# Closing the sample's 32 tokens in two column halves, behind the last prompt tile's closing multiply

## The chip, the core and the metric

The kernel runs on one core of one Trainium2 chip. The metric is the time of one execution on the device in microseconds (us); less is better. The core's engines work side by side and wait for each other through semaphores: PE (TensorE, matrix products), DVE (VectorE), ACT (ScalarE), POOL (GpSimd), and SP, which issues most of the DMA transfers between HBM and SBUF, the on-chip memory. SBUF has 128 partitions; an address here is a byte offset within a partition.

## The reference: what is computed

Two groups of tokens go through two mixer layers with shared weights: 4096 prompt frames and 32 sample frames of width 1024. Each layer adds a gated mixer output to the residual x, and a final RMSNorm closes both groups:

```python
def trunk(x, c, conv_st, gla_st, pool_st, pos0, ...):
    for l in range(DEPTH):                       # DEPTH = 2
        h = rms_norm(x, norm_g[l]) * (1.0 + scale[:, None, :]) + shift[:, None, :]
        if l % 2 == 0:
            y, cb, gs = even_mixer(h, ...)       # conv branch and gated linear recurrence, w_out
        else:
            y, pb = pool_mixer(h, ...)           # trailing means, gate, then @ w_out
        x = x + gate[:, None, :] * y
    return rms_norm(x, final_g), ...

def rms_norm(x, g):
    y = x * lax.rsqrt(jnp.mean(x * x, axis=-1, keepdims=True) + EPS)
    return y * g
```

The change concerns the last two steps for the 32 sample frames: `x + gate * y` and the final `rms_norm`.

## The kernel before

**Tiles and stages.** The 4128 tokens are cut into 11 blocks: ten of 384 prompt tokens and a last one of 256 prompt and 32 sample tokens. The program goes through stages, each over all blocks: A (first input projection, conv branch; matmul results in `psA`), B (recurrence branch; `psv`, `psg`, `psk`, `psq`), C (first output projection; `psC`), D (second input projection and pooling; `psD`), E (second output projection and final norm; `psE`). Intermediate results go through HBM between the stages.

**Float32 products in three passes.** Every float32 operand is split into a high part and a low part of the rounded type f32r, and a product is the sum of three matmuls (`PASS`). In stages A and D, and for `psg`, `psk`, `psq` of B, `gemm_B` (L162) holds a 128x128 piece of the weights `w` in PE and streams the activation tile `h[k]` (384 columns, or 288 in the last block) past it: 8 tiles k times 3 passes are 24 matmuls for one result tile. The profile's names give the streamed operand first: `psD<-h,w_du` streams `h`, `psE<-w_e,op` streams the weights `w_e`, with `op` held. In `psv`, `psC` and `psE` the weights are streamed and the activations are held.

**Where the tiles lie.** SBUF is handed out by pools, one behind the other, each as large as its tags need: `cst`, `wp`, `stg`, `sm`, then `hp` (whose 12 buffers hold the tiles `h`, `hB`, `hC`), then the pools of the stages (`A`; `B` and `B1`; `xp`; `C`; `D`; `E`, which takes over the place of `hp` too). The pools `A2`, `CE` and `X0` are opened with `side="right"` and placed from the end of SBUF. `sm` holds the small per-token sums (`ss`, `r`, `rt1`, ...). Each tile's buffer begins at a multiple of 32 bytes. Two tags of activations lie outside `hp`: the tiles k = 6 and 7 of every block in stage A (pool `A`, `split_h` with `(ap_, 3)`), and the tiles k = 6 and 7 of blocks 1 to 9 in stage B (pool `B1`, tag `hx`, L147 and L1010). Block 0 in stage B has all eight in `hp`.

**The end of the program.** In stage E, `add` and `finish` (L1404) close the prompt tiles in pairs: DVE adds the products to `xE`, ACT squares the row with a running sum, POOL makes the reciprocal root in two instructions (`rstd_pool`, L213), and the rest of `finish`, a DVE multiply by root and weight (L1413) and the output DMA on SP's queue (L1414), comes when `flush()` is called. Stage E runs in an order tied by `keep_in_program_order` for the matmuls, ACT's `act` and the DVE instructions inside `pin`; instructions outside these are placed by the scheduler. After the last pair, a loop over two column halves nh does the sample: 16 matmuls into `psES`, `sum_S` (L208: an ACT copy and a DVE add), a DVE multiply by the gate `gS` (L1509), a DVE add to `xS` (L1510); `flush()` stands at the end of the loop body. Then `finish` runs once over all 1024 columns of `xS`.

Of the kernel before, what the change touches and what calls it, by code (L numbers as in the profile page):

```python
# [8 lines left out]
F32 = mybir.dt.float32  # L9
F32R = mybir.dt.float32r  # L10
BF16 = mybir.dt.bfloat16
U8 = mybir.dt.uint8
AF = mybir.ActivationFunctionType
ALU = mybir.AluOpType
PSUM = bass.MemoryType.PSUM

P = 128
D = 1024
# [12 lines left out]
def trunk(  # L31
# [8 lines left out]
    nc = tc.nc  # L40
    L = x_prompt.shape[1]
    NS = x_sample.shape[1]
# [26 lines left out]
    LB = blocks[-1]  # L69
# [4 lines left out]
    def rows(ap_p, ap_s, blk, c0, n, seq):  # L74
        if seq:
            return ap_s[0, 0:n, :]
        return ap_p[0, blk.start + c0:blk.start + c0 + n, :]
# [5 lines left out]
    sm = ctx.enter_context(tc.tile_pool(name="sm", bufs=3))  # L83
# [6 lines left out]
    def mm(shape, name):  # L90
        t = pp.tile(shape, F32, tag=f"m{turn['m']}", name=name, bufs=2)
        turn["m"] = (turn["m"] + 1) % 3
        return t
# [67 lines left out]
    def pin(ins):  # L161
        if PIN["dve"]:  # L162
            tc.keep_in_program_order(ins)

    def mmul(*args, **kw):
        ins = nc.tensor.matmul(*args, **kw)  # L166
        if PIN["on"]:
            tc.keep_in_program_order(ins)
# [6 lines left out]
    def act(*args, **kw):  # L175
        ins = nc.scalar.activation(*args, **kw)  # L176
        if PIN["act"]:
            tc.keep_in_program_order(ins)
# [34 lines left out]
    def rstd_pool(out, ss, n, m, inv, name):  # L213

        t = sm.tile([P, m], F32, tag=f"rt{m}", name=f"rt_{name}")
        nc.gpsimd.tensor_scalar(out=t[:n], in0=ss, scalar1=inv, scalar2=EPS, op0=ALU.mult, op1=ALU.add)  # L216
        nc.gpsimd.tensor_tensor(out=out, in0=t[:n], in1=mhalf[:n, 0:m], op=ALU.pow)  # L217
# [214 lines left out]
    with tc.tile_pool(name="A", bufs=2, reuse_waits="tile") as ap_:  # L432
# [166 lines left out]
        for blk in blocks:  # L599
# [4 lines left out]
            for idx, (kind, c, col) in enumerate(order):  # L604
# [14 lines left out]
                elif kind == "val":  # L619
# [8 lines left out]
                    for (c0, m, seq) in blk.segs:  # L628
                        if seq:
# [3 lines left out]
                                                       in1=av[:, c0:c0 + m], op0=ALU.add, op1=ALU.mult)  # L633
# [103 lines left out]
    with ExitStack() as bctx:  # L737
# [7 lines left out]
        for r in range(4):  # L745
            t = bp.tile([P, 2, P], F32, name=f"attm{r}")
# [160 lines left out]
        for blk in blocks:  # L907
# [25 lines left out]
            for (i0, i1, m) in ([(0, nsub, P)] if not blk.last else [(i, i + 1, sb[1]) for i, sb in enumerate(blk.subs)]):  # L933
# [3 lines left out]
                                        in1=lrs[:m, i0:i1, 0, :].bitcast(F32), op=ALU.subtract)  # L937
# [31 lines left out]
            for j in range(2):  # L969
# [5 lines left out]
                                                 op0=ALU.add, op1=ALU.min)  # L975
# [12 lines left out]
            for i, (c0, m, seq) in enumerate(blk.subs):  # L988
# [3 lines left out]
                                        in1=la.to_broadcast([P, 2, m]), op=ALU.subtract)  # L992
# [93 lines left out]
    with tc.tile_pool(name="C", bufs=2, reuse_waits="tile") as cp:  # L1086
# [37 lines left out]
        for blk in blocks:  # L1124
# [10 lines left out]
            for u, (i, nh) in enumerate(units):  # L1135
# [7 lines left out]
                t = cp.tile([P, 512], F32, tag="pg", name=f"pgC{blk.i}_{i}{nh}")  # L1143
                if seq:
                    sum_S(t[:m], ps, m)
                pg_ins = nc.vector.tensor_tensor(out=t[:m], in0=t[:m] if seq else ps[:m], in1=grow[:m, seq, cols],
                                                 op=ALU.mult)
                nc.vector.tensor_tensor(out=xt[:m, cols], in0=t[:m], in1=xt[:m, cols], op=ALU.add)
                if nh == 1:
                    nc.sync.dma_start(x1D[blk.i][i], xt[:m])  # L1150
                    junk = cp.tile([P, 512], F32, tag="pg", name=f"junkC{blk.i}_{i}").bitcast(BF16)
# [120 lines left out]
    with tc.tile_pool(name="D", bufs=2, reuse_waits="tile") as dp:  # L1272
# [3 lines left out]
        for blk in blocks:  # L1276
# [3 lines left out]
            for idx, (kind, j) in enumerate(dord):  # L1280
# [6 lines left out]
                if kind == "u":  # L1287
# [14 lines left out]
                    while step < wn:  # L1302
                        t = dp.tile([P, UW], F32, tag="s", name=f"s{blk.i}_{j}_{step}")
# [6 lines left out]
                                                   in1=u[:, PP:off], op0=ALU.mult, op1=ALU.subtract)  # L1310
# [4 lines left out]
                else:  # L1315
# [3 lines left out]
                    for (c0, m, seq) in blk.segs:  # L1319
                        a = PP + c0 + (PP if seq else 0)  # L1320
                        nc.vector.scalar_tensor_tensor(out=y1[:, c0:c0 + m], in0=pt[:, a:a + m], scalar=gbs[:, j:j + 1],  # L1321
                                                       in1=sgt[:, c0:c0 + m], op0=ALU.add, op1=ALU.mult)
# [14 lines left out]
    with tc.tile_pool(name="E", bufs=2, reuse_waits="tile") as ep:  # L1337
# [4 lines left out]
        fg = ep.tile([P, D], F32, name="fg", bufs=1)  # L1342
# [19 lines left out]
        def load_xE(p):  # L1362
            xs = []
            for r, (b, i, c0) in enumerate(pairs[p]):
                xt = ep.tile([P, D], F32, tag="x", name=f"xE{p}_{r}", bufs=4)
                (nc.sync if p else nc.gpsimd).dma_start(xt, x1D[b.i][i])
                xs.append(xt)
            return xs
# [28 lines left out]
        def prod(ps, left, i, first):  # L1397
            m = 0
            for k in range(4):
                for (hi, wi) in PASS:  # L1400
                    mmul(ps, left.ops[i][:, hi, k, :], wE[PROD[i], k // 2][:, wi, k % 2, :],
                         start=bool(first) and m == 0, stop=m == 11,
                         skip_group_check=not first)
                    m += 1  # L1404

        def finish(xt, n, name, dst):
            junk = ep.tile([P, D], BF16, tag="junk", name=f"junk{name}", bufs=1)
            ss = sm.tile([P, 1], F32, tag="ss", name=f"ss{name}")
            act(junk[:n], xt[:n], AF.Square, accum_out=ss[:n])
            r = sm.tile([P, 1], F32, tag="r", name=f"r{name}")  # L1410
            rstd_pool(r[:n], ss[:n], n, 1, 1.0 / D, name)
            yield
            pin(nc.vector.scalar_tensor_tensor(out=xt[:n], in0=xt[:n], scalar=r[:n], in1=fg[:n], op0=ALU.mult, op1=ALU.mult))  # L1413
            nc.sync.dma_start(dst, xt[:n])  # L1414
# [3 lines left out]
        def flush():  # L1418
            for g in ends:
                list(g)  # L1420
            ends.clear()

        H = (slice(0, 512), slice(512, 1024))
# [18 lines left out]
        for p in range(len(pairs)):  # L1442
            more = p + 1 < len(pairs)
            nxt = nxs = None
            if p > 0 and more:
                nxt, nxs = Left(p + 1), load_xE(p + 1)
            x1, x2 = xs
            bank = [mm([P, 512], f"psE{p}_{q}") for q in range(3)]

            def add(x, h, ps):  # L1450
                pin(nc.vector.tensor_tensor(out=x[:, H[h]], in0=ps, in1=x[:, H[h]], op=ALU.add))  # L1451


            for i, (q, first, adds) in enumerate(((0, 1, (x1, 0)), (1, 1, (x1, 0)), (0, 0, (x1, 1)), (2, 1, (x2, 1)),
                                                  (0, 0, (x2, 1)), (2, 0, (x1, 1)), (0, 0, (x2, 0)))):
                prod(bank[q], cur, i, first)
                add(*adds, bank[q])
                flush()
                if i >= 5:
                    b, _, c0 = pairs[p][i - 5]  # L1460
                    ends.append(finish(xs[i - 5], P, f"E{p}_{i - 5}", rows(y_prompt, y_sample, b, c0, P, 0)))
                    next(ends[-1])
                if p == 0:

                    if i < 4:
                        cur.make(i + 3)
                    if i == 0:
                        lateE.pop(0)(), lateE.pop(0)()
                        nxt = Left(1)
                        nc.sync.dma_start(fg, final_g.partition_broadcast(P))  # L1470
                    if i in (2, 3):
                        lateE.pop(0)()
                    if i == 3:
                        nxs = load_xE(1)
                    for j in ((), (), (), (0,), (1, 2), (3,), (4,))[i]:
                        nxt.make(j)
                    continue
                if p == 1 and i < 2:
                    cur.make(i + 5)
                if more:  # L1480
                    nxt.make(i)
                else:
                    load_S(i)
                    if i == 6:
                        load_S(7)
                if not more and i == 2:

                    ysr = stg.tile([P, KT, MH], F32, tag="st", name="ys")
                    nc.sync.dma_start(ysr, y1D[LB.i][:, :, LB.np:LB.n])
                    hS = ep.tile([P, KT, 3 * MH], F32R, tag="op", name="hS", bufs=8)  # L1490
                    nc.scalar.activation(hS[:, :, 0:MH], ysr, AF.Copy)
                    for q in (1, 2):
                        nc.vector.tensor_tensor(out=hS[:, :, q * MH:(q + 1) * MH], in0=ysr,
                                                in1=hS[:, :, 0:MH].bitcast(F32), op=ALU.subtract)
                    xS = ep.tile([P, D], F32, tag="x", name="xS", bufs=4)
                    nc.sync.dma_start(xS[:NS], x1D[LB.i][len(LB.subs) - 1])
                    gS = ep.tile([P, D], F32, tag="x", name="gS", bufs=4)
                    nc.sync.dma_start(gS[:NS], gateD[1][1, :].partition_broadcast(NS))
            cur, xs = nxt, nxs
        for nh in range(2):  # L1500
            ps = mm([P, 512], f"psES{nh}")
            m = 0
            for k in range(KT):
                for wi in range(2):
                    mmul(ps[:3 * MH], hS[:, k, :], wS[nh, k // 2][:, wi, k % 2, :], start=(m == 0), stop=(m == 2 * KT - 1))
                    m += 1
            t = ep.tile([P, 512], F32, tag="S", name=f"tS{nh}", bufs=4)
            sum_S(t[:NS], ps, NS)
            nc.vector.tensor_tensor(out=t[:NS], in0=t[:NS], in1=gS[:NS, H[nh]], op=ALU.mult)  # L1509
            nc.vector.tensor_tensor(out=xS[:NS, H[nh]], in0=t[:NS], in1=xS[:NS, H[nh]], op=ALU.add)  # L1510
            flush()
        list(finish(xS, NS, "ES", rows(y_prompt, y_sample, LB, LB.np, NS, 1)))


_INS = ["x_prompt", "x_sample", "c_prompt", "c_sample", "state_conv", "state_gla", "state_pool",
# [29 lines left out]
```

## Time and profile before

| | |
|---|---|
| median of 3 runs | 2864.99 us (2864.03 to 2866.5) |
| the profiled execution's own time | 2866.98 us |
| its span | 2865.3 us, in which PE is busy 2812.4 us, DVE 1959.7 us, ACT 1023.9 us |
| granted PE clock, mean | 0.994 |
| stages, by the first matmul of each | A from 62 us, B from 639 us, C from 1346 us, D from 1779 us, E from 2535 us |
| last matmul starts, last DVE instruction starts, last DMA is issued | 2854.24 us, 2861.12 us, 2862.42 us |

Times within a profile count from the span's start. The span covers the instructions that the profiler recorded; the execution's own time is 1.68 us longer. "x24" behind a row is a count of instructions; the duration of such a row reaches from the start of its first instruction to the end of its last.

### The profile page before, as it was taken

What the parts mean: (1) busy time and instruction counts of PE and PEld (TensorE: products, weight loads), DVE (VectorE), ACT (ScalarE), POOL (GpSimd) and SP (SyncE); (2) the same over time, 40 slices, a digit from 0 to 9 for tenths busy, and PEclk for the clock granted to TensorE, in tenths of its full rate; (3) what the DMA queues carried; (4) which work ended last, traced back from release to release, by engine and by line L of the source; (5) the groups of instructions that cost most, each with busy time, mean ns of one, the idle gap of its engine ahead of it and who ended that gap; (6) DMA issues with size and microseconds to landing.
All of it is one profiled execution on the core that took longest, in us unless ns stands there. A gap on an engine that the chain in (4) does not pass through costs nothing. (4 is left out here: it accounts for less than half of the span.)

```text
span 2865.3 us, 43285 instructions
## 1 busy us (share of the span) xinstructions
PE 2812.4 (98%) x16593; PEld 2612.3 (91%) x16593; DVE 1959.7 (68%) x3907; ACT 1023.9 (36%) x2137; POOL 247.1 (9%) x492
## 2 busy tenths in 40 slices
PE   7999999999999999998999999999999999999998
PEld 5999999999999999997878887999999999988886
DVE  4997886888878888886866674533333333577776
ACT  5434334334334334334232224422222323343333
POOL 1110000000000000011111110001111110000000
PEclk9999999999999999999999999999999999999999
DMA  8523323233111111115455554312222221365544
GB/s 290 156 87 106 105 95 106 78 112 91 59 51 49 45 45 57 48 47 185 168 195 184 191 194 139 125 62 69 73 71 71 69 71 51 116 204 176 164 159 155
DMA packets 249667, 323.70 MB, mean 113 GB/s; under 512 B 18793, under 2 KB 198907, under 8 KB 248947
## 3 DMA queue, kind: packets, MB, share of 16 engines
q1 hardware_dynamic: 248635, 318.78, 34.2%
q8 instruction: 130, 2.13, 0.3%
q0 software_dynamic: 704, 2.11, 0.2%
q14 instruction: 78, 0.64, 0.1%
q10 hardware_dynamic: 120, 0.04, 0.0%
HBM read 211.21 MB, written 109.65 MB: 112 GB/s over the span
## 5 line engine op out<-in xcount | busy, mean ns | idle before, releaser
L166 PE MATMUL psC<-w_c,hC 128*128 128x512 f32 (+1 forms) x1568 | 377.0, 397 | 0.0
L166 PE MATMUL psD<-h,w_du 128*128 128x384 f32 (+1 forms) x2112 | 376.6, 332 | 0.1
L166 PE MATMUL psD<-h,w_dg 128*128 128x384 f32 (+1 forms) x2112 | 376.4, 332 | 0.0
L417 DVE SCALAR_TENSOR_TENSOR co<-g,cwt,co 128x384 f32<-128x384 f32 (+1 forms) x660 | 370.1, 605 | 4.9
L166 PEld LDWEIGHTS psD<-h,w_du 128*128 128x128 f32 x2112 | 357.8, 188 | 1.0 <-DVE h L152 0.4
L166 PEld LDWEIGHTS psD<-h,w_dg 128*128 128x128 f32 x2112 | 357.8, 188 | 0.5
L166 PEld LDWEIGHTS psC<-w_c,hC 128*128 128x128 f32 (+1 forms) x1568 | 292.9, 189 | 60.7
L417 DVE SCALAR_TENSOR_TENSOR coB<-glB,cwt,coB 128x384 f32<-128x384 f32 x600 | 333.1, 610 | 0.0
L166 PE MATMUL psE<-w_e,op 128*128 128x512 f32 x1344 | 307.6, 391 | 4.2 <-DVE xE L1451 2.4
L166 PEld LDWEIGHTS psE<-w_e,op 128*128 128x128 f32 x1344 | 253.0, 189 | 58.6 <-issue 3.2
L166 PE MATMUL psv<-w_wv,hB 128*128 128x264 f32 (+1 forms) x1568 | 207.3, 288 | 2.0 <-ACT vt L891 2.0
L166 PEld LDWEIGHTS psv<-w_wv,hB 128*128 128x128 f32 (+1 forms) x1568 | 195.0, 188 | 5.0 <-ACT vt L891 2.4
L166 PE MATMUL psg<-hB,w_bg 128*128 128x384 f32 (+1 forms) x1056 | 189.5, 336 | 3.2 <-ACT vt L891 1.5
L166 PE MATMUL psA<-h,w_aglu 128*128 128x384 f32 (+1 forms) x1056 | 190.4, 333 | 0.2
L166 PE MATMUL psA<-h,w_aval 128*128 128x384 f32 (+1 forms) x1056 | 189.1, 333 | 0.0
L166 PE MATMUL psA<-h,w_agate 128*128 128x384 f32 (+1 forms) x1056 | 187.2, 333 | 0.0
L1300 DVE COPY halo<-u 128x15 f32<-128x15 f32 x80 | 14.1, 177 | 252.6 <-ACT u L1296 252.6
L166 PEld LDWEIGHTS psg<-hB,w_bg 128*128 128x128 f32 x1056 | 181.1, 189 | 4.2 <-ACT vt L891 1.8
L166 PEld LDWEIGHTS psA<-h,w_aglu 128*128 128x128 f32 x1056 | 178.8, 188 | 2.7 <-issue 1.7
L166 PEld LDWEIGHTS psA<-h,w_aval 128*128 128x128 f32 x1056 | 178.3, 188 | 0.1
L166 PEld LDWEIGHTS psA<-h,w_agate 128*128 128x128 f32 x1056 | 178.0, 188 | 0.1
L1321 DVE SCALAR_TENSOR_TENSOR sgD<-p,gbs,sgD 128x384 f32<-128x384 f32 (+1 forms) x96 | 56.3, 593 | 124.9 <-ACT sgD L1317 123.8
(268 smaller groups left out, 3720.3 us busy)
## 6 DMA issues: line engine op xcount, KB each, us to landing
x<-in_x_prompt SPq DMA_DIRECT2D x64, 512.0 KB
aw<-in_ada_w SPq DMA_DIRECT2D x32, 512.0 KB
x1D<-x SPq DMA_DIRECT2D x32, 512.0 KB
x<-x1D SPq DMA_DIRECT2D x32, 512.0 KB
out<-xE SPq DMA_DIRECT2D x32, 512.0 KB
hfD<-hf_a SPq DMA_DIRECT2D x80, 192.0 KB
hfB<-hfD SPq DMA_DIRECT2D x40, 384.0 KB
y1D<-sgD SPq DMA_DIRECT2D x80, 192.0 KB
```

The lines of the kernel that those rows point to most:

```text
L166: ins = nc.tensor.matmul(*args, **kw)
L417: nc.vector.scalar_tensor_tensor(out=out[:, :w], in0=src[:, j:j + w], scalar=cwt[:, c, j:j + 1], in1=out[:, :w], op0=ALU.mult, op1=ALU.add)
L1300: nc.vector.tensor_copy(halo[:, j, :], u[:, TB:TB + PP])
L1321: nc.vector.scalar_tensor_tensor(out=y1[:, c0:c0 + m], in0=pt[:, a:a + m], scalar=gbs[:, j:j + 1], in1=sgt[:, c0:c0 + m], op0=ALU.add, op1 ...
```

## The change

```diff
@@ after the loop over the pairs of stage E @@
             cur, xs = nxt, nxs
+        flush()
+        ssS = sm.tile([P, 2], F32, tag="ssS", name="ssS", bufs=1)
         for nh in range(2):
             ps = mm([P, 512], f"psES{nh}")
...
             sum_S(t[:NS], ps, NS)
             nc.vector.tensor_tensor(out=t[:NS], in0=t[:NS], in1=gS[:NS, H[nh]], op=ALU.mult)
             nc.vector.tensor_tensor(out=xS[:NS, H[nh]], in0=t[:NS], in1=xS[:NS, H[nh]], op=ALU.add)
-            flush()
-        list(finish(xS, NS, "ES", rows(y_prompt, y_sample, LB, LB.np, NS, 1)))
+
+            junk = ep.tile([P, D], BF16, tag="junk", name=f"junkES{nh}", bufs=1)
+            act(junk[:NS, 0:512], xS[:NS, H[nh]], AF.Square, accum_out=ssS[:NS, nh:nh + 1])
+        r = sm.tile([P, 1], F32, tag="r", name="rES")
+        t = sm.tile([P, 1], F32, tag="rt1", name="rt_ES")
+        nc.vector.tensor_tensor(out=t[:NS], in0=ssS[:NS, 0:1], in1=ssS[:NS, 1:2], op=ALU.add)
+        rstd_pool(r[:NS], t[:NS], NS, 1, 1.0 / D, "ES")
+        for nh in range(2):
+            nc.vector.scalar_tensor_tensor(out=xS[:NS, H[nh]], in0=xS[:NS, H[nh]], scalar=r[:NS], in1=fg[:NS, H[nh]],
+                                           op0=ALU.mult, op1=ALU.mult)
+            (nc.sync, nc.scalar)[nh].dma_start(rows(y_prompt, y_sample, LB, LB.np, NS, 1)[:, H[nh]], xS[:NS, H[nh]])
```

The squares and the closing multiply of the sample go by halves of 512 columns, the two half sums are added by DVE, and the output leaves in two DMAs, the first from SP's queue and the second from ACT's. `flush()` moves ahead of the loop. The new tile `ssS` is a tag of its own in `sm`.

At the end of DVE's queue the rows stood as follows before (`xE_1` is the second tile of the last prompt pair, `w_s` a split of the sample's weights, the two `tS` are the halves nh = 0 and 1).

```order
L119 TENSOR_TENSOR w_s_27735<-st_s_27733,w_s_27735 128x1024
L211 TENSOR_TENSOR tS_27755<-psES_27738,tS_27755 32x512
L1509 TENSOR_TENSOR tS_27755<-tS_27755,gS 32x512
L1510 TENSOR_TENSOR xS<-tS_27755,xS 32x512
L1413 SCALAR_TENSOR_TENSOR xE_1_27433<-xE_1_27433,rE_1_27724,fg 128x1024
L211 TENSOR_TENSOR tS_27779<-psES_27762,tS_27779 32x512
L1509 TENSOR_TENSOR tS_27779<-tS_27779,gS 32x512
L1510 TENSOR_TENSOR xS<-tS_27779,xS 32x512
L1413 SCALAR_TENSOR_TENSOR xS<-xS,rES,fg 32x1024
```

With the change the same place of DVE's queue holds these rows.

```order
L119 TENSOR_TENSOR w_s_27735<-st_s_27733,w_s_27735 128x1024
L1413 SCALAR_TENSOR_TENSOR xE_1_27433<-xE_1_27433,rE_1_27724,fg 128x1024
L211 TENSOR_TENSOR tS_27758<-psES_27741,tS_27758 32x512
L211 TENSOR_TENSOR tS_27782<-psES_27765,tS_27782 32x512
L1511 TENSOR_TENSOR tS_27758<-tS_27758,gS 32x512
L1511 TENSOR_TENSOR tS_27782<-tS_27782,gS 32x512
L1512 TENSOR_TENSOR xS<-tS_27758,xS 32x512
L1512 TENSOR_TENSOR xS<-tS_27782,xS 32x512
L1518 TENSOR_TENSOR rt_ES<-ssS 32x1
L1521 SCALAR_TENSOR_TENSOR xS<-xS,rES,fg 32x512 x2
```

The multiply of `xE_1` moved ahead of all work of the sample, the two halves now alternate instead of following each other, and one 32x1 add stands between the squares and the closing multiplies.

At the end of ACT's queue the rows with the change are these (the last row before them, the split of `w_s`, is the same as before).

```order
L176 ACTIVATE w_s_27735<-st_s_27733 128x1024
L210 ACTIVATE tS_27758<-psES_27741 32x512
L210 ACTIVATE tS_27782<-psES_27765 32x512
L176 ACTIVATE junkES_27763,ssS<-xS 32x512
L176 ACTIVATE junkES_27787,ssS<-xS 32x512
L1523 DMA out<-xS 32x512
```

Before, one 32x1024 square stood in place of the last three rows. On no engine does any other instruction change its place.

The new tag makes the pool `sm` 32 bytes larger per partition, and the pools placed behind it begin 32 bytes later. This is where the program lays them, and the remainder of the address by 64:

| tiles | pool | address before | by 64 | with the change | by 64 |
|---|---|---|---|---|---|
| `h`, `hB`, `hC` (12 buffers of 3072 bytes) | `hp` | 134336 and on | 0 | 134368 and on | 32 |
| `h`, k = 6, 7 in stage A | `A` | 198848, 201920, 204992 | 0 | 32 more | 32 |
| `hB`, k = 6, 7 of blocks 1 to 9 in stage B | `B1` | 212000, 215072 | 32 | 32 more | 0 |
| `w_e` of the last product (2 of its 14 tiles), `op`, `xE` | `E` | | 0 | 32 more | 32 |
| `x` | `xp` | | 0 | 32 more | 32 |
| `w_*` | `wp` | | 0 | the same | 0 |
| staging tiles of the loads | `stg` | | 0 | the same | 0 |

The low half of each `h` tile begins 1536 bytes, 24 times 64, behind the high half.

## The prediction

> **What bounds the kernel now.** I read the page's busy times first, then the busy times by stage (the windows view), the groups of matmuls, and last the timeline: first the end of the program, where the edit stands, then the matmul rows of stages A, B and D, whose operands the edit moves in memory.
>
> ```profile
> span 2865.3 us, 43285 instructions
> 62.00:639.00 577.00, 575.12 (x3442) 564.57 (x3443) 472.40 (x945) 231.40 (x411) 36.86 (x59) 1.00 0.33 109
> 639.00:1346.00 707.00, 694.43 (x5015) 662.40 (x5013) 591.81 (x1263) 279.04 (x823) 53.12 (x72) 1.00 0.21 64
> 1346.00:1779.00 433.00, 425.03 (x2017) 349.44 (x2018) 293.69 (x536) 125.06 (x227) 56.33 (x124) 0.98 0.54 181
> 1779.00:2534.00 755.00, 754.51 (x4500) 747.06 (x4498) 329.81 (x734) 244.97 (x433) 65.53 (x133) 1.00 0.26 84
> 2534.00:2855.00 321.00, 315.67 (x1376) 258.00 (x1376) 237.30 (x339) 112.34 (x192) 24.65 (x65) 0.99 0.54 172
> ```
>
> The five rows are stages A to E: the stretch and its length, then the busy time of PE, its weight loads, DVE, ACT and POOL, then clock, DMA share and GB/s. PE is busy 575.12 of 577 us in A, 694.43 of 707 in B and 754.51 of 755 in D. DVE, the next, has 105 us free in A and 115 in B. So whatever makes PE's matmuls slower in A, B and D goes into the time almost one to one, and the edit at the end can only act on the last 11 us, where PE is done.
>
> **The end of the program.** The timeline there (start, duration, engine, line, operands):
>
> ```profile
> 2852.21 0.59 ACT L210 ACTIVATE tS<-psES 32x512 f32<-32x512 f32 x1
> 2853.55 0.67 DVE L211 TENSOR_TENSOR tS<-psES,tS 32x512 f32<-32x512 f32 x1
> 2854.26 0.68 DVE L1509 TENSOR_TENSOR tS<-tS,gS 32x512 f32<-32x512 f32 x1
> 2854.67 0.59 ACT L210 ACTIVATE tS<-psES 32x512 f32<-32x512 f32 x1 [1.87 <-PE psES L166]
> 2854.97 0.68 DVE L1510 TENSOR_TENSOR xS<-tS,xS 32x512 f32<-32x512 f32 x1
> 2855.58 1.27 DVE L1413 SCALAR_TENSOR_TENSOR xE<-xE,rE,fg 128x1024 f32<-128x1024 f32 x1
> 2856.78 0.67 DVE L211 TENSOR_TENSOR tS<-psES,tS 32x512 f32<-32x512 f32 x1
> 2858.20 0.68 DVE L1510 TENSOR_TENSOR xS<-tS,xS 32x512 f32<-32x512 f32 x1
> 2859.05 1.05 ACT L176 ACTIVATE junkES<-xS 32x1024 bf16<-32x1024 f32 x1 [3.79 <-DVE xS L1510]
> 2860.01 0.18 ACT L176 ACTIVATION_READ_ACCUMULATOR junkES<-xS 32x1 f32 x1
> 2860.28 0.18 POOL L216 TENSOR_SCALAR rt_ES<-ssES 32x1 f32<-32x1 f32 x1 [9.08 <-ACT junkES L176]
> 2861.12 1.27 DVE L1413 SCALAR_TENSOR_TENSOR xS<-xS,rES,fg 32x1024 f32<-32x1024 f32 x1 [2.24 <-POOL rES L217]
> 2862.42 0.33 SPq L1414 DMA_DIRECT2D out<-xS  x1
> L1314 DVE TENSOR_TENSOR p<-p,u 128x1 f32<-128x1 f32 x2 | 0.3, 161 | 0.1
> 2.73 0.61 ACTq L447 DMA_DIRECT2D vr<-in_ev_conv_b  x1
> ```
>
> DVE works without a pause from 2853.55 to 2858.88 on seven instructions; then come ACT's square, POOL's root, DVE's multiply and the DMA, each waiting for the one before. The change keeps the seven instructions and only orders them anew, so putting `xE_1` in front moves no work off this path. A neighbour that needs the result before it starts 0.71 us later (2853.55 to 2854.26), one that doesn't 0.61 (2854.97 to 2855.58), and behind the long multiply 1.20 (2855.58 to 2856.78). With the halves alternating, every neighbour is independent: the last add starts at 2853.55 + 1.20 + 5 x 0.61 = 2857.80 and ends at 2858.48, **0.40 earlier**. The second `tS` needs ACT's copy, which ends at 2855.26, and its turn comes at 2855.36, so no new wait.
>
> The squares: a half is costed like the 32x512 ACT copy, 0.59, with 0.18 for the accumulator. The first starts at 2857.87 + 0.17 (the hop from 2858.88 to 2859.05) = 2858.04 and is read out by 2858.73; the second follows and is read out by about 2859.43 instead of 2860.19. The new 32x1 add costs 0.16 by the 128x1 row, with some 0.15 of hops, so POOL starts at about 2859.76 instead of 2860.28, and DVE's first half multiply at 2860.60. Its halves start 0.61 apart; the second ends at 2861.89 instead of 2862.39. The second DMA waits on ACT's queue, behind which nothing stands; this trace has ACT issues of up to 0.61 against SP's 0.33. The sum is **-0.5 us** plus up to 0.3 for the issue and 0.14 for the hop; I take **-0.4**. The bounds: +0.6, if ACT's half squares cost as much again in fixed time, and -1.3, one whole closing multiply. Moving `flush()` also ends the multiply of `xE_1` at 2854.82 instead of 2856.85 and lets its output leave 2 us sooner, further ahead of the sample's; I count nothing for it.
>
> **The operands that move.** The 8-byte tile `ssS` shifts every pool behind `sm` by 32 bytes. No streamed `h` tile of stages A and D started off a multiple of 64 before; with the change all of them do. The trace has the same case already, in stage B: block 0 streams eight `hB` tiles from `hp` (multiples of 64), blocks 1 to 9 stream six from there and the tiles k = 6, 7 from `B1` (32 off).
>
> ```profile
> 677.29 8.48 PE L166 MATMUL psk<-hB,w_k 128*128 128x384 f32 x48
> 685.61 8.48 PE L166 MATMUL psq<-hB,w_q 128*128 128x384 f32 x48
> 740.41 8.52 PE L166 MATMUL psk<-hB,w_k 128*128 128x384 f32 x48
> 1065.00 8.52 PE L166 MATMUL psq<-hB,w_q 128*128 128x384 f32 x48
> 227.13 4.32 PE L166 MATMUL psA<-h,w_aval 128*128 128x384 f32 x24
> 2000.41 4.32 PE L166 MATMUL psD<-h,w_dg 128*128 128x384 f32 x24
> ```
>
> The first two rows are block 0: 48 matmuls back to back in 8.48 us. The next two are the first and the last of twelve such rows of blocks 1 to 6, all 8.52. The only difference is that 12 of the 48 stream from `B1`: 0.04 / 12 = **3.3 ns each**, 2.5 to 4.2 by what rounding leaves (0.03 to 0.05). Distance from `hp` does not explain it: the `psA` row streams 6 of its 24 from pool `A` at 198848 and above, on a multiple of 64, and takes the 4.32 of the `psD` row, which streams from `hp` alone.
>
> ```profile
> L166 PE MATMUL psD<-h,w_du 128*128 128x384 f32 (+1 forms) x2112 | 376.6, 332 | 0.1
> L166 PE MATMUL psD<-h,w_dg 128*128 128x384 f32 (+1 forms) x2112 | 376.4, 332 | 0.0
> L166 PE MATMUL psA<-h,w_aglu 128*128 128x384 f32 (+1 forms) x1056 | 190.4, 333 | 0.2
> L166 PE MATMUL psA<-h,w_aval 128*128 128x384 f32 (+1 forms) x1056 | 189.1, 333 | 0.0
> L166 PE MATMUL psA<-h,w_agate 128*128 128x384 f32 (+1 forms) x1056 | 187.2, 333 | 0.0
> L166 PE MATMUL psg<-hB,w_bg 128*128 128x384 f32 (+1 forms) x1056 | 189.5, 336 | 3.2 <-ACT vt L891 1.5
> L166 PE MATMUL psk<-hB,w_k 128*128 128x384 f32 (+1 forms) x528 | 92.1, 332 | 0.2 <-ACT bg L954 0.2
> L166 PE MATMUL psq<-hB,w_q 128*128 128x384 f32 (+1 forms) x528 | 93.5, 336 | 0.0
> ```
>
> `psA` and `psD` are 3 x 1056 + 2 x 2112 = 7392 matmuls, all shifted off 64: 7392 x 3.3 = 24.4 us. `psg`, `psk`, `psq` are 2112; 192 in each of 11 blocks. In blocks 1 to 9 a quarter, 432, streams from `B1` and comes onto 64: -1.4. The other 1680 go off: +5.5. Of `psE`, 12 of 84 matmuls per pair stream from the two `w_e` tiles in pool `E`, 192 in all: +0.8 at the columns' ratio 512/384. `psv` and `psC` stream weights from `wp`, which stays, and hold the activations; I count nothing there. The 288-column forms are counted like the others, some 0.7 too much, and PE's few waits in B take about as much: -1.1 in all. The sum is 24.4 - 1.4 + 5.5 + 0.8 - 1.1 = **+28.2 us**. By 2.5 ns it is 21, by 4.2 it is 36; below stands nothing (a shift that costs PE nothing), and no row gives a reason for a gain. DVE, ACT and DMA operands shift too; I cost them at nothing because PE covers them (DVE 83% busy in A), and they would count only from some 100 us of extra DVE work.
>
> Against the profiled execution: 2866.98 + 28.2 - 0.4 = 2894.8. That execution lies 2.0 above the median of the runs, so for a median I forecast **2893 us**, 28 us or 1.0% more.
>
> [...]
>
> **The rivals.** *A smaller price per matmul* (2871 to 2883): `B1` lies 32 bytes behind a multiple of 128, while `hp` goes from 64 to 96 behind one. If the price hangs on more address bits than I can see, half of 3.3 ns is as good a guess as any: 2893 - 14 = 2879. Against it: nothing measured; for it: only one shifted address pair is in the trace. *No price at all, the edit does only what it says*: the 0.04 us of blocks 1 to 6 would come from something else in `B1`, such as traffic of the other tiles there; it takes the place of my forecast if pool `A`'s 4.32 row says nothing of stage B. Then the time is 2865.0 - 0.4 = 2864.6, not slower. *A dearer one* (2896 to 2903): 12 of 48 matmuls sit in pairs of tiles, and if the price lies in going from one shifted tile to the next, eight in a row pay it seven times where two pay it once; then 4.2 ns or more each hold, 2865 + 36 = 2901.
>
> **How the numbers follow.** Forecast (2884 to 2896) 0.60; smaller price 0.12; dearer 0.13; no price 0.15. The range takes in the first three, **2872 to 2901**, and leaves out no price and the edges. About 0.2% (6 us) is what a measurement of this kernel can tell from no change. Slower by more than that: 0.83; within: 0.16, which is no price and a very small one; faster: 0.01.
>
> **What would show it.** Right: `psA` and `psD` rows of 24 at 4.39 to 4.42 instead of 4.32, `psk` of block 0 at about 8.64 and of block 1 at about 8.60, each stage A and D longer by about 10 to 14 us, C unchanged; the end 0.4 us shorter from the last matmul on. Wrong: 4.32 and 8.48 as before, and the whole difference in the last 11 us.

## The result, and the profile after

The changed kernel takes 2885.66 us (median of 6 runs, 2880.54 to 2887.09), the kernel before 2865.74 beside it (6 runs, 2863.4 to 2869.78): a ratio of 1.0064, 95% interval 1.0054 to 1.0074. It is 19.9 us slower. Forecast were 28 us, with a range that holds the measured time.

The profiled execution took 2886.64 us. This is the head of its page and its busy times by stage (the windows view, columns as before, cut where the first matmul of each stage starts):

```profile
span 2884.9 us, 43292 instructions
62.00:640.30 578.30, 576.05 (x3447) 565.51 (x3446) 472.90 (x946) 232.57 (x411) 36.16 (x59) 1.00 0.33 109
640.30:1349.00 708.70, 697.12 (x5014) 665.11 (x5012) 591.25 (x1262) 278.32 (x823) 51.14 (x72) 0.99 0.21 64
1349.00:1787.50 438.50, 432.39 (x2017) 349.57 (x2017) 293.54 (x535) 125.37 (x227) 56.30 (x124) 0.98 0.53 179
1787.50:2548.30 760.80, 759.35 (x4500) 752.12 (x4498) 330.34 (x736) 246.07 (x436) 66.06 (x134) 1.00 0.25 84
2548.30:2874.30 326.00, 322.86 (x1376) 258.21 (x1376) 236.33 (x335) 111.10 (x189) 24.13 (x64) 0.99 0.53 169
```

DVE, ACT and POOL are busy as long as before in every stage, within 2.0 us. PE is busier: +0.9 us in A, +2.7 in B, +7.4 in C, +4.8 in D, +7.2 in the last stretch, 23.0 in all. The matmuls are the same, and the clock column is the same in every row but B's (0.99 against 1.00), so outside B the matmuls take on average longer at the same clock. PE's pauses shrank by 3.7 us in all, worked out from the same rows (in C from 7.97 to 6.11, for one), which leaves 19.3 of the span's 19.6.

The stages' lengths, from the first matmul of one to the first of the next (E ends at the first `psES`):

| us | A | B | C | D | E | from there to the last record |
|---|---|---|---|---|---|---|
| before | 577.44 | 707.07 | 432.86 | 755.76 | 310.58 | 19.69 |
| after | 578.36 | 708.91 | 438.57 | 760.77 | 317.93 | 18.72 |
| difference | +0.9 | +1.8 | +5.7 | +5.0 | +7.4 | -1.0 |

With the start 0.2 us earlier these add up to the span's 19.6. Two thirds of the loss lie in C and E, where almost none was forecast. The groups by form name the matmuls there (busy us, mean ns of one, then idle time ahead of them); first before, then after:

```profile
L166 PE MATMUL psC<-w_c,hC 128*128 128x512 f32 x1536 | 369.1, 397 | 0.0
L166 PE MATMUL psE<-w_e,op 128*128 128x512 f32 x1344 | 307.6, 391 | 4.2 <-DVE xE L1451 2.4 <-ACT op L176 1.8
```

```profile
L166 PE MATMUL psC<-w_c,hC 128*128 128x512 f32 x1536 | 376.7, 402 | 0.0
L166 PE MATMUL psE<-w_e,op 128*128 128x512 f32 x1344 | 315.4, 397 | 3.7 <-DVE xE L1451 2.3 <-ACT op L176 1.4
```

Each group grew by about 7.7 us. In the timeline a stretch of 24 `psC` matmuls, undisturbed, shows the pace (start, duration); first before, then after:

```profile
1482.92 5.82 PE L166 MATMUL psC<-w_c,hC 128*128 128x512 f32 x24
```

```profile
1486.64 5.94 PE L166 MATMUL psC<-w_c,hC 128*128 128x512 f32 x24
```

0.12 us over 24 is 5 ns more for each. Start to start, the back-to-back `psC` matmuls average 227.6 ns before and 233.0 after, those of `psE` whose weights lie in `wp` 226.7 and 233.2.

The rows that the prediction named, in the changed kernel's timeline:

```profile
227.13 4.32 PE L166 MATMUL psA<-h,w_aval 128*128 128x384 f32 x24
677.37 8.48 PE L166 MATMUL psk<-hB,w_k 128*128 128x384 f32 x48
740.49 8.63 PE L166 MATMUL psk<-hB,w_k 128*128 128x384 f32 x48
...
1919.31 4.32 PE L166 MATMUL psD<-h,w_du 128*128 128x384 f32 x24
1923.47 4.32 PE L166 MATMUL psD<-h,w_dg 128*128 128x384 f32 x24
1927.63 4.40 PE L166 MATMUL psD<-h,w_du 128*128 128x384 f32 x24
...
1948.83 4.41 PE L166 MATMUL psD<-h,w_dg 128*128 128x384 f32 x24
```

`psA` keeps its 4.32, `psk` of block 0 its 8.48. `psk` of block 1 has 8.63. Each block of D has sixteen groups of 24 (indices 0 to 15). The four `psD` rows are indices 14 and 15 of one block, at 4.32, and the first and the last of the next block's 0 to 5, at 4.40 and 4.41: (4.40 - 4.32) / 24 = 3.3 ns more per matmul. So 3.3 ns is a size that occurs, at far fewer places than forecast.

The end of the program after (timeline):

```profile
2873.62 1.28 DVE L1413 SCALAR_TENSOR_TENSOR xE<-xE,rE,fg 128x1024 f32<-128x1024 f32 x1
2874.72 0.59 ACT L210 ACTIVATE tS<-psES 32x512 f32<-32x512 f32 x1 [1.84 <-PE psES L166]
2874.82 1.27 DVE L211 TENSOR_TENSOR tS<-psES,tS 32x512 f32<-32x512 f32 x2
...
2877.22 1.27 DVE L1512 TENSOR_TENSOR xS<-tS,xS 32x512 f32<-32x512 f32 x2
2877.97 0.63 ACT L176 ACTIVATE junkES<-xS 32x512 bf16<-32x512 f32 x1 [2.66 <-DVE xS L1512]
...
2879.26 0.18 ACT L176 ACTIVATION_READ_ACCUMULATOR junkES<-xS 32x1 f32 x1
2879.48 0.15 DVE L1518 TENSOR_TENSOR rt_ES<-ssS 32x1 f32<-32x1 f32 x1 [0.98 <-ACT junkES L176]
2879.71 0.18 POOL L216 TENSOR_SCALAR rt_ES<-rt_ES 32x1 f32<-32x1 f32 x1 [8.44 <-DVE rt_ES L1518]
2880.55 1.40 DVE L1521 SCALAR_TENSOR_TENSOR xS<-xS,rES,fg 32x512 f32<-32x512 f32 x2 [0.93 <-POOL rES L217]
2881.99 0.34 ACTq L1523 DMA_DIRECT2D out<-xS  x1
```

From the second `tS` copy to the last DMA issue it is 2881.99 - 2874.72 = 7.27 us; before, 2862.42 - 2854.67 = 7.75. The edit's own work is 0.48 shorter.

### The profile page after: what moved, and what is told of

Its sections match the earlier page's. It is cut to its first block, busy times and chain, and to the rows that moved or that the text cites. A ratio compares the mean times of both kernels' runs of the same rounds, so it can differ in the third digit from the quotient of the medians.

```text
span 2884.9 us, 43292 instructions
## 1 busy us (share of the span) xinstructions
PE 2837.1 (98%) x16593; PEld 2621.9 (91%) x16593; DVE 1960.0 (68%) x3909; ACT 1025.1 (36%) x2139; POOL 241.9 (8%) x492
## 5 line engine op out<-in xcount | busy, mean ns | idle before, releaser
L166 PE MATMUL psC<-w_c,hC 128*128 128x512 f32 (+1 forms) x1568 | 384.5, 402 | 0.0
L166 PE MATMUL psE<-w_e,op 128*128 128x512 f32 x1344 | 315.4, 397 | 3.7 <-DVE xE L1451 2.3
```

## The experiments

Two facts of the layout are needed to read them. First, the start of each tile by 256, the remainder that turned out to matter. In the kernel before, the weights in `wp`, the activations in `hp`, the `h` tiles k = 6, 7 in pool `A`, the weights in pool `D` and the operands in `E` all leave 192 (`hp` begins at 134336 = 524 x 256 + 192); only `hB` k = 6, 7 in `B1` leaves 32. The change takes everything behind `sm` to 224, `B1` to 64, and leaves `wp` at 192. The slices that a matmul takes from a tile keep its remainder, but for `psv`, which streams slices of 1056 bytes, and the 32 `psES`. Second, which operand is where: `psA`, `psD`, `psg`, `psk`, `psq` stream activations and hold weights; `psv`, `psC` and `psE` stream weights and hold activations.

The differences of stage lengths below are against the 577.44, 707.07, 432.86, 755.76 and 310.58 above. Before, e3, e9, e10 and e11, which all lay `wp`, `hp`, `D` and `E` alike, spread over 2.0 us in A, 3.4 in B, 2.0 in C, 1.7 in D and 0.3 in E. So E can be read to half a microsecond and D to two; A, B and C need their matmul rows beside them.

### Pad the new tile to 64 bytes (e1), shift without the edit (e2), shift both operands (e3), shift weights by 32 and activations by 64 (e4)

The forecast's theory blames the streamed operand: it pays when its start is off a multiple of 64. Its rival blames the pair: a matmul pays when its two operands no longer leave the same remainder. A third possibility is that the edit's own instructions cost the time.

```diff
 e1: the changed kernel, with
-    ssS = sm.tile([P, 2], F32, tag="ssS", name="ssS", bufs=1)
+    ssS = sm.tile([P, 16], F32, tag="ssS", name="ssS", bufs=1)
 e2: the kernel before, with an unused tile at the start of sm
+    sm.tile([P, 8], F32, tag="pad", name="pad_sm", bufs=1)
 e3: the kernel before, with an unused tile at the start of cst, ahead of wp
+    cst.tile([P, 8], F32, name="pad_cst")
 e4: the kernel before, with both unused tiles
```

> The changed kernel with ssS made 64 bytes instead of 8, so that every pool behind sm begins 64 bytes later than before, on the remainders by 64 that it had before. Theory 'addresses' (the 20 us come from where the tiles lie): stages A to E as long as before, the end as short as with the change, about 2865 us, ratio 0.9997. Rival 'instructions' (the new rows at the end, or their DMA on ACT's queue, cost the 20 us): 2885 us, ratio 1.007.

> The kernel before with nothing but an unused 32-byte tile in sm; no instruction differs. Theory 'addresses': the stages as with the change (A +1, B +2, C +6, D +5, E +7 us), the end as before, about 2886 us, ratio 1.007. Rival 'instructions': 2865.7 us, ratio 1.000.

> The kernel before with an unused 32-byte tile in cst, the first pool, so that wp (the weights), stg, sm, hp and all stage pools begin 32 bytes later together. Streamed and held operands lie 32 off a multiple of 64, both. Theory 'pair' (a matmul pays when its streamed and its held operand have different remainders by 64): psC and psE at 227 ns from one start to the next, psD at 173, 2866 us, ratio 1.000. Rival 'streamed' (my prediction's: a matmul pays when its streamed operand is off a multiple of 64): C and E are now off too, 233 ns there and 177 in parts of D, 2886 us or more, ratio 1.007.

> The kernel before with 32 unused bytes in cst and 32 in sm: the weights in wp lie 32 off a multiple of 64, hp and the stage pools on one. Theory 'pair': the same pairs differ as with the change, so C +6, D +5, E +7, B about +2 us, 2886 us, ratio 1.007. Rival 'streamed': A and D stream h from multiples of 64 and stay at 173 ns, only C and E, which stream the weights, pay: +13 us, 2879 us, ratio 1.0046. Rival 'held' (a matmul pays when its held operand is off): A and D pay, C and E don't, +5 to +7 us, 2872 us.

Measured:

| | `wp` by 256 | `hp`, `A`, `C`, `D`, `E` | us | ratio to before (95%) | A | B | C | D | E |
|---|---|---|---|---|---|---|---|---|---|
| e1 | 192 | 0 | 2876.73 | 1.0034 (1.0022 to 1.0047) | -0.3 | -0.8 | +5.1 | +0.3 | +7.1 |
| e2 | 192 | 224 | 2886.61 | 1.0074 (1.0059 to 1.0088) | +2.9 | +2.5 | +5.1 | +5.4 | +7.4 |
| e3 | 224 | 224 | 2867.04 | 0.9998 (0.9989 to 1.0007) | +1.5 | -1.8 | +0.4 | 0.0 | 0.0 |
| e4 | 224 | 0 | 2886.93 | 1.0072 (1.0056 to 1.0087) | +2.2 | +0.7 | +4.3 | +4.6 | +7.1 |

e2 changes no instruction and costs what the change costs: the shift is the cause, and the edit's own work isn't. (Its stage lengths are those of its longest execution, 2892.3 us, at a mean granted clock of 0.992 instead of 0.994; so its A and B are read with care.) e3 is the decisive one. All activations lie on the same shifted addresses as in e2, off a multiple of 64, and nothing is paid, because the weights were shifted with them. In e4 activations lie on multiples of 64, weights do not, and the cost is back. So it is not the streamed operand's own address that counts, but **how the two operands of a matmul lie to each other**. The groups by form say so of `psC` and `psE`; e3 first, then e4:

```profile
L167 PE MATMUL psC<-w_c,hC 128*128 128x512 f32 x1536 | 369.7, 397 | 0.1
L167 PE MATMUL psE<-w_e,op 128*128 128x512 f32 x1344 | 307.6, 391 | 4.2 <-DVE xE L1452 2.4 <-ACT op L177 1.8
```

```profile
L168 PE MATMUL psC<-w_c,hC 128*128 128x512 f32 x1536 | 377.5, 403 | 0.0
L168 PE MATMUL psE<-w_e,op 128*128 128x512 f32 x1344 | 314.4, 395 | 4.5 <-DVE xE L1453 3.0 <-ACT op L178 1.4
```

e1 is a miss of every theory so far: with the operands 64 apart the 384-column matmuls of A and D run at their old pace (the `psA` row of 24 takes 4.32 us, stage D is 0.3 us longer), and the 512-column ones of C and E pay in full (by form `psC` is busy 377.4 us and `psE` 315.2, before 369.1 and 307.6). So the two kinds of matmul don't pay at the same distances. They differ in width and also in which operand is streamed, and no run separates these two.

### How far apart: 128 bytes (e5, e6), 96 (e7), 256 (e11)

With the pair established, the question is the modulus: 128 or 256.

```diff
 the changed kernel, with
+    ssS = sm.tile([P, 32], F32, tag="ssS", name="ssS", bufs=1)     # e5, e6: 128 bytes
+    ssS = sm.tile([P, 24], F32, tag="ssS", name="ssS", bufs=1)     # e7: 96 bytes
+    ssS = sm.tile([P, 64], F32, tag="ssS", name="ssS", bufs=1)     # e11: 256 bytes
 e6: in addition an unused tile at the start of B1
+        b1.tile([P, 8], F32, tag="pad", name="pad_b1", bufs=1)
```

> The changed kernel with ssS made 128 bytes, so that hp and the pools behind it begin 128 bytes later than in the kernel before. e1 (64 bytes) left A, B and D at their old length but kept C at +5 and E at +7 us. Theory 'pair by 128' (the remainders that count are those by 128): C and E are back at 227 ns per matmul, 433 and 311 us, and only the end's gain of about 0.9 us is left: 0.9997 of before. Rival 'pair by 256 or more': C and E stay at 233 ns, +10 us, ratio 1.0034.

> As e5, and B1 moved 32 bytes further, so that its two hB buffers have the same remainder by 128 as the weights and hp. Theory 'pair by 128': besides what e5 gives, psk and psq of blocks 1 to 9 come from 174.0 to 173.3 ns (rows of 48 from 8.52 to 8.48 us) and psg likewise, stage B about 1.5 to 2 us shorter than before: ratio 0.999. If only the streamed operand's own remainder counted, B1 would be as good at any multiple of 64; rows of 8.48 then too, so this run tells the gain and not the theories.

> ssS made 96 bytes: hp and the pools behind begin 96 bytes later, which is 32 short of 128. Theory 'pair by 128': 96 is as far from an equal remainder as 32, from the other side, and the stages cost as with the change: C +6, E +7, D up to +5, B +2 us. If the held operand lying behind the streamed one matters and not the distance, C and E differ from +6 and +7 clearly.

> ssS made 256 bytes: hp and all pools behind it begin 256 bytes later. Theory 'pair by 256': all remainders by 256 are those of before, so all stages are as before, ratio 0.9997. Rival 'the distance itself, or remainders by more than 256': C and E stay at 233 ns, A and D are dear as with 128 bytes (176 ns), ratio 1.003 to 1.009.

Measured, with the distance from weights in `wp` to activations:

| | bytes apart | us | ratio to before (95%) | A | B | C | D | E |
|---|---|---|---|---|---|---|---|---|
| e5 | 128 | 2894.41 | 1.0094 (1.0078 to 1.0109) | +6.4 | +0.2 | +4.3 | +7.5 | +6.8 |
| e6 | 128, `B1` equal | 2891.73 | 1.0078 (1.0066 to 1.0091) | +5.5 | +0.2 | +4.9 | +7.7 | +6.8 |
| e7 | 96 | 2897.22 | one run | +9.5 | +3.1 | +2.3 | +9.0 | +7.7 |
| e11 | 256 | 2866.97 | 0.9998 (0.9987 to 1.0009) | +2.0 | -0.4 | -1.6 | 0.0 | -0.1 |

"Equal by 128" falls with e5, which is dearer than the change. "Equal by 256" holds in e11: same edit, same instructions, no loss. e6 misses its expectation: the `psk` and `psq` rows of blocks 1 to 9 take 8.59 us, not 8.48, and B keeps its length. e7 was expected to cost what the change costs; A and D pay 9.5 and 9.0 us. Rows of the same place of stage A, timeline; e5, then e7, then e11:

```profile
227.58 4.38 PE L166 MATMUL psA<-h,w_aval 128*128 128x384 f32 x24
```

```profile
229.76 4.40 PE L166 MATMUL psA<-h,w_aval 128*128 128x384 f32 x24
```

```profile
230.87 4.32 PE L166 MATMUL psA<-h,w_aval 128*128 128x384 f32 x24
```

At 96 bytes the 384-column matmuls of A, and those of D whose weights lie in `wp`, are all as dear as I had forecast for 32 bytes. And `psC` of e11 is back:

```profile
L166 PE MATMUL psC<-w_c,hC 128*128 128x512 f32 x1536 | 368.4, 396 | 0.0
L166 PE MATMUL psE<-w_e,op 128*128 128x512 f32 x1344 | 307.4, 391 | 4.3 <-DVE xE L1451 2.5 <-ACT op L176 1.8
```

### Why D pays at 32 bytes and A hardly does (e8, e12)

In the changed kernel indices 0 to 5 of a D block are slow (176.7 ns from start to start), 6 to 15 are not (173.3 to 173.6, and about 174.6 at index 12). Indices 0 to 11 hold weights of `wp`, 32 apart from `h`; 12 to 15 hold weights of pool `D`, which moved with `h`. Index 0 of a block follows directly on index 15 of the one before; behind index 5 transposes stand between the groups. Either the equal operands of 12 to 15, or the switch from one distance to another, could be what makes 0 to 5 slow.

```diff
 the changed kernel, with an unused tile at the start of pool D
     with tc.tile_pool(name="D", bufs=2, reuse_waits="tile") as dp:
+        dp.tile([P, 8], F32, tag="pad", name="pad_d", bufs=1)      # e8: 32 bytes
+        dp.tile([P, 56], F32, tag="pad", name="pad_d", bufs=1)     # e12: 224 bytes
```

> The changed kernel with 32 unused bytes at the start of pool D, so that the four weight tiles kept there (indices 12 to 15 of stage D) no longer have the remainder of hp but one 32 bytes on. With the change, indices 0 to 5 of blocks 1 to 9 run at 176.7 ns right behind indices 12 to 15 at 173 to 174, and 6 to 11, each behind three transposes, at 173.3 to 173.6. Theory 'each unequal pair is able to run at either pace and keeps the one that it entered with': 12 to 15 now are unequal too, so the run from 12 over the block's end to 5 keeps one pace, either 176.7 for all ten (D +3 us more) or 173.3 for all (D -5 us, as before the change). Rival 'the equal pairs are what cures': 0 to 5 stay at 176.7 and 12 to 15 join them.

> The changed kernel with 224 unused bytes at the start of pool D: the weights there get the remainder by 256 of those in wp, so that all 16 weights of stage D differ from h by the same 32 bytes. Theory 'an unequal pair can run at either pace, and a switch between pairs of different distance without a pause is what throws it into the slow one': no switch from index 15 to 0 any more, so 0 to 5 stay at 173.3 ns as in stage A and D is back at 756 us. Rival 'wp weights with h 32 bytes on are slow in stage D as such': 0 to 5 at 176.7, D 761 us or more.

e8, one run: 2885.42 us. `D` weights leave 0, `h` 224. Indices 12 to 15 are now 32 apart as well, and stay at 173.3 to 174.1; 0 to 5 of blocks 1 to 9 stay at 176.5 to 176.7. Neither theory's wording holds: being unequal isn't enough to be slow, and equality at 12 to 15 isn't what makes 0 to 5 slow. But the 32 bytes have two directions here: `h` lies 32 behind the weights of `wp` and 32 ahead of those of `D`, so a switch from one distance to another remains at index 0.

e12, one run: 2885.75 us. `D` weights leave 192 like `wp`, so that all sixteen indices have the same distance. Indices 0 to 5 of blocks 1 to 9 now run at 173.3, as the first theory expected, and only those of block 0, entered from stage C, at 176.8 (and index 6 of block 9 at 176.7). D is 757.27 long, 3.5 less than in the change. Timeline of e12, two of those indices:

```profile
1939.90 4.32 PE L166 MATMUL psD<-h,w_dg 128*128 128x384 f32 x24
1944.06 4.32 PE L166 MATMUL psD<-h,w_du 128*128 128x384 f32 x24
```

So at 32 bytes the 384-column matmuls have two paces (about 173.3 and 176.7 ns from start to start), and mostly keep the one they are in from group to group. Blocks 1 to 9 of D fit one description: they fall into the slow pace where matmuls of one distance follow directly on those of another, and leave it where transposes stand between. It does not cover everything. In the changed kernel six groups of A are slow though all of A lies 32 apart: in block 2 the pace turns slow right behind a fast group of the same distance. And block 0 of D starts slow behind transposes in the changed kernel and in e12, and fast in e8. The time of this one run lies only 0.9 us below the change's profiled 2886.64: its A came out 1.6 us longer and its end, behind the last stage, 2.7, and nothing in the edit touches either. So the rows show the effect on D, and no gain in time is shown.

### The edit without the shift (e9), and the one old unequal pair made equal (e10)

```diff
 e9: the changed kernel, with the sums in a tag of sm that is large enough
-    ssS = sm.tile([P, 2], F32, tag="ssS", name="ssS", bufs=1)
+    ssS = sm.tile([P, 2], F32, tag="bna", name="ssS")
 e10: e9, with an unused tile at the start of B1, so that hB k = 6, 7 leaves 192
+        b1.tile([P, 40], F32, tag="pad", name="pad_b1", bufs=1)
```

> The changed kernel with ssS put into the tag bna of sm, which has room: the same instructions in the same order as with the change, every address as before it. Theory 'pair' (a matmul pays when its streamed and its held operand have different remainders; by which power of two is open, since 64 and 128 were not enough): all stages as in the kernel before, only the end 0.7 to 1 us shorter, ratio 0.9997, and not distinguishable from 1. Rival 'instructions': 1.007.

> As e9, and 160 unused bytes at the start of B1, so that hB for k = 6, 7 has the remainder of hp and of the weights by 256. Theory 'pair': the last unequal pairs of B are gone, psk and psq rows of 48 in blocks 1 to 9 at 8.48 instead of 8.52 us, psg likewise, stage B 1 to 2 us shorter: about 2.5 us below before, ratio 0.9991. Rival (the 8.52 came from B1's place, not its remainder): 8.52 stays.

e9 issues the change's instructions in the same order on every engine, on the addresses of before: 2866.62 us (11 runs) against 2867.5, ratio 1.0001 (0.9992 to 1.001). The loss is gone. Its end (timeline) keeps the edit's gain:

```profile
2854.69 0.59 ACT L210 ACTIVATE tS<-psES 32x512 f32<-32x512 f32 x1 [1.87 <-PE psES L166]
...
2861.92 0.34 ACTq L1523 DMA_DIRECT2D out<-xS  x1
```

That is 7.23 us where before has 7.75; 0.7 to 1 us less was expected. Half a microsecond is 0.02% of the time, too little for the runs to tell.

e10: 2866.64 us, ratio 0.9998 (0.9989 to 1.0006). Block 1's `psk`, timeline:

```profile
740.54 8.48 PE L166 MATMUL psk<-hB,w_k 128*128 128x384 f32 x48
```

It is at block 0's 8.48 instead of 8.52, as expected. This settles what the prediction had read in those rows: their 0.04 us came from `B1` lying 96 by 256 from the weights, and `hp` from lying equal with them. The gain in time is again below what can be told. No version beat the kernel before.

## Why the prediction was right, and where it was not

**That PE sets the time and a slower matmul goes in almost whole: right.** PE's added 23.0 us, less the 3.7 by which its pauses shrank, are the loss. (DVE, given as 83% busy in A, is 472.40 of 577 us busy, 82%; nothing hangs on it.)

**That the 8-byte tile costs, by 32 bytes of shift, and not the edit's steps: right**, by e2 (shift alone, 1.0074) and e9 (edit alone, 1.0001).

**The end: right.** -0.48 measured, -0.5 worked out and -0.4 taken. DVE's seven instructions, from the first one's start to the last one's end, go from 5.33 us (2853.55 to 2858.88) to 4.87 (2873.62 to 2878.49): -0.46 for -0.40. The squares, from the last add to the read-out, go from 1.31 to 0.95, as worked out. The add and its hops take 0.27 where one hop took 0.09. The two half multiplies take 1.40 for 1.27.

**The step that failed is the one on which matmuls pay**: that those do whose streamed operand starts off a multiple of 64 ("all shifted off 64: 7392 x 3.3 = 24.4 us"), and with it "`psv` and `psC` stream weights from `wp`, which stays, and hold the activations; I count nothing there". e3 refutes the first and e1 to e4 the second. The row had shown that `B1` differs from `hp`. I compared each with a round number, and not with the other operand of the same matmul, whose remainder stood in the same table. The `psA` row that streams from `A` and `hp` alike fitted both readings.

Its terms, sized anew. For A, B and D the measure is the sum of the start-to-start times of consecutive matmuls of one result, below 200 ns, against the same sum before:

| term | forecast | measured | why |
|---|---|---|---|
| `psA` | 3168 x 3.3 = +10.5 | +0.6 | all 32 apart, but only six of its 120 groups of 384 columns are in the slow pace; 0.5 of it comes from the 288-column block |
| `psD` | 4224 x 3.3 = +13.9 | +5.2 | slow in indices 0 to 5 of ten blocks: 60 x 24 x 3.3 ns = 4.8; the 288-column block has the rest |
| `psg`, `psk`, `psq` | +4.1 | +1.9 | `psk` and `psq` of blocks 1 to 9 at 8.63 for 8.52; `psg` unchanged; block 0 stays at 8.48 |
| `psC` | 0 | +5.7 (stage C) | 512 columns pay at every distance tried that isn't 0 by 256: 32, 64, 96, 128 (stage C +5.7, +5.1, +2.3, +4.3) |
| `psE` | +0.8 | +7.4 (stage E) | as `psC`; the two `w_e` tiles in pool `E`, which moved along with `op`, are those that pay least: 230.6 ns for the first, which follows directly on unequal ones, 226.7 for the second |

A, B and D were forecast 20.8 us too dear by these terms, C and E 12.3 too cheap. So it is luck that the total came within 8 us of the forecast: two errors, each larger than that, had opposite signs. Of the signs that the prediction named, `psA` at 4.39, block 0's `psk` at 8.64, A and D longer by 10 to 14 us each and "C unchanged" did not show; block 1's `psk` (8.60 named, 8.63 seen), 4.40 in a part of D, and the end did.

**The rivals.** "No price at all" falls with e2. "A smaller price per matmul" comes as near in time (2879) as the forecast and is wrong as a mechanism: it thought of one smaller price for the same matmuls. "A dearer one" has nothing for it at 32 bytes; 96 and 128 bytes are dearer, since there A pays too (+9.5 us in e7, +6.4 in e5).

**What stays open.** The runs show that the difference by 256 counts (256 bytes apart 0.9998 of before in e11, 128 apart 1.0094 in e5); no row shows which part of the chip makes it so. The two paces at 32 bytes are described, not explained: why a switch of distance brings the slow one, and why 64 bytes leaves the 384 columns of A alone (rows of 24 at 4.32 us in e1) while 96 slows them all (4.40 in e7), was not found. The switch itself rests on e8 and e12, one run each, and on the same pattern in the trace of the change; the slow groups of A and of D's block 0 do not follow from it.

## What to carry to other kernels

A new tile, however small, can move every pool behind it: before pricing an edit, list which tiles change their address, and for each hot matmul compare the start of the streamed operand with that of the held one; here equal remainders by 256 were the fast case (e3 and e11: 0.9998 of before). A small tile is best put into a tag that has room, as in e9. And where one row shows a price for an address, ask what else differs between the two cases, the other operand first, before multiplying it by thousands.

## What the runs showed that I had not expected

- A 512-column matmul takes on average 226.7 to 227.9 ns from start to start where its two operands leave the same remainder by 256 and no unequal ones precede, and 232.7 to 234.2 where they are 32, 64, 96 or 128 bytes apart (the change, e1, e7, e5). In e1, where these alone pay, the ratio is 1.0034.
- A 384-column matmul takes about 173.3 ns from start to start at 0 and at 64 bytes (before, e1), 175.5 to 176.2 at 128 (e5), 176.7 at 96 in A and D (e7), and either 173.3 or 176.7 at 32 (the change). These are distances with the activations behind the weights. The other direction is not the same: with `hB` in `B1` 96 bytes ahead of the weights the `psk` rows of e1 take 8.48 us, where 96 bytes behind, in the kernel before, they take 8.52. The 512-column matmuls were tried only with the activations behind. The 264-column `psv` has its slices at all eight multiples of 32 from the held operand already in the kernel before, and its pace does not follow the distance: at 32 bytes it averages 122.4 ns there and 125.4 with the change.
- e2 and e3 have the same streamed addresses in A and D and the same held ones in C and E, and differ by 19.6 us (2886.61 against 2867.04).
